# The order and the rate at which a hybrid mixer's projections are traced between its head chains

## The chip, the cores and the metric

One core of one Trainium2 chip runs the whole program. The metric is the device time in microseconds (us) of one execution; lower is better. The engines are named PE (TensorE, the matrix engine), DVE (VectorE), ACT (ScalarE), POOL (GpSimd) and SP (SyncE, which here only issues DMAs).

## The reference

A trunk of two layers over 512 positions of width 1024. Each layer is a SwiGLU feed-forward block (FFN) at half weight, a mixer, and a second FFN, each with a norm before and after and with shift, scale and gate from a conditioning vector. The mixer, the part that matters here, is:

```python
def hybrid_mixer(h, w_in, ...):
    proj = h @ w_in                                   # q, k, v, z, beta, a, u
    qkv = silu(causal_dwconv(qkv, conv_w))            # 4 taps along the sequence
    q, k = l2_normalize(heads(q)), l2_normalize(heads(k))
    o = chunked_gated_delta_rule(q, k, v, beta, g)    # 4 heads of 128, chunks of 64
    y_gdn = rms_norm(o, gdn_norm_w) * silu(z)
    y_s5 = s5_mixer(u, ...)                           # diagonal complex scan, 32 groups of 16 channels
    return concatenate([y_gdn, y_s5]) @ w_out

def chunked_gated_delta_rule(...):                    # per head and chunk
    system = lower_triangular(kb @ k.T * decay) + I
    w_val, k_cum = solve(system, [vb, kb * exp(g)])
    attn = q @ k.T * decay
    # then over the chunks, in order:
    v_new = w_val - k_cum @ S;  o = q @ S + attn @ v_new;  S = S * exp(g_last) + k.T @ v_new

def s5_mixer(u, ...):
    x = scan(abar, bbar @ u)                          # complex, along the sequence
    y = gelu(Re(c @ x) + d * u)
    return y * sigmoid(y @ w_glu)
```

## The kernel before

The kernel is written in a tile framework: it is traced as a program of tile operations, and a scheduler puts each engine's instructions into one order, in which what was traced earlier has priority. Each engine then takes its instructions in that order and waits where an input is not there.

fp32 precision in the wide matmuls comes from splitting each operand into a high and a low part in a reduced type: weight `wh`, `wl` and activation `..hh`, `..hl`. Three matmuls (L266 to L268: high by high, high by low, low by high) make one product of 128 rows by 512 positions, 24 of them one projection of 128 columns. `Weights.get` hands out the weights in the order in which they are packed, and prepares those that are next: a DMA on SP of 128x1024 into one of four raw buffers, two casts on ACT (L223) for `wh`, two subtractions for `wl` on DVE (L231) or, for 10 of a mixer's 30 weights, on POOL. So the DMA of a weight waits until the low part of the fourth weight before it is made.

A mixer (`mixer`, L1165) projects heads 0 and 1 first (L1199 to L1219). Then three kinds of work are traced in an interleaved way:

- `main1` (L1293) yields the projections that are left, in the order of the string `ORDER` (L48): `u` is the input of S5 (four groups of 24 matmuls, `m0u0` to `m0u3`, copied to `utc`, 16 steps), `2` and `3` are q, k, v of heads 2 and 3 (`m0p20` to `m0p32`, 12 steps each), each followed by its convolution over four taps (`conv`: one ACT copy, three DVE operations, SiLU on ACT). A step is 6 matmuls. The host packs the weights by the same string.
- `main2` (L1299) follows: z of the four heads (16 steps, `m0z0` to `m0z3`), then, when all of S5's outputs are traced, its gate matmuls (`m0gl0` to `m0gl3`), and, when the first heads' outputs are traced, the output projection (`m0od`).
- The chains: the decay factors (`gen_decay`), two head pairs (`gen_pair`: pair 0 is heads 0 and 1, pair 1 heads 2 and 3) and three S5 generators (`gen_s5`, four channel groups s0 to s3, the last by whichever is free first).

Names in the chains: `pu` and `pa` are the products k k^T and q k^T of a head (L941), `U` and `at` what ACT and DVE make of them, `g0` and `g1` the solve of pair 0 and pair 1. A solve is 15 forward substitution steps on DVE (L1004 shuffle, L1005 multiply, L1006 add, over `xs` and `xb`), for blocks of 16, and then merges of blocks on PE (`pp`, `px`, `pt`), with transposes on DVE (L1015, L1032) and copies on ACT between them. `pk` uses the solved block, `pb` are the matmuls of the recurrence over chunks, `S` the state (L1156 on DVE), `pon` the transposes of the heads' outputs. In S5 `vr` and `vi` are the input products, L849 to L854 and L860, L863 the products and the scans on DVE, `y` the output matmuls.

The loop at the end of `mixer` (L1349 on) sets how they are interleaved: in each round every active chain is advanced by one yield, and the projections by the number of steps that the table in L1357 adds to `acc`: nine in `main1`, one in `main2` until the fourth z is traced, two after it. Pair 1 joins the chains when v of head 2 has been traced (`(2 * started, 2) in qkv`).

Of the kernel before, what the change touches and what calls it, by code (L numbers as in the profile page):

```python
# [44 lines left out]
C_BD = 640  # L45
C_BS = 672
C_LV = 704
ORDER = "2u3"  # L48
C_GM = 736
C_E = C_GM + 2  # L50
NCST = C_E + BASE
# [3 lines left out]
def trunk(ctx: ExitStack, tc: tile.TileContext, x_d, c, wmod, wun, vecs, wab, s5p, cst_d, out, depth=2):  # L55
# [1113 lines left out]
    def mixer(l, h):  # L1169
# [87 lines left out]
        zs = [None] * 4  # L1257
# [7 lines left out]
        def main_u():  # L1265
            wu = [W.get(3 - i) for i in range(4)]
            tt = [slot(f"{name}utc{ch}") for ch in range(4)]
            for t in range(4):
                pu = mmps(f"{name}u{t}")
                for k in range(KD):  # L1270
                    hi, lo = wu[k // 2][0][k % 2], wu[k // 2][1][k % 2]
                    ht = [hh[:, t:T:4] for hh in h[k]]
                    PE.matmul(pu, ht[0], hi, start=k == 0, stop=False)
                    PE.matmul(pu, ht[1], hi, start=False, stop=False)
                    PE.matmul(pu, ht[0], lo, start=False, stop=k == KD - 1)
                    if k % 2:
                        yield
                for ch in range(4):
                    ACT.copy(tt[ch].rearrange("p (a t h) -> p t a h", a=8, t=4)[:, t],
                             q4(pu)[:, ch].rearrange("p (a h) -> p a h", a=8))  # L1280
            utc[:] = tt

        def main_qkv(hd):
            for i in range(3):
                w = W.get(3)
                ps = mmps(f"{name}p{hd}{i}")
                for k in range(KD):
                    mm3(ps, w, k, h[k], FULL, k == 0, k == KD - 1)
                    if k % 2:
                        yield  # L1290
                qkv[hd, i] = conv(slot(f"{name}c{hd}{i}"), ps, 4 * i + hd)

        def main1():  # L1293
            for i in ORDER:
                yield from main_u() if i == "u" else main_qkv(int(i))
# [52 lines left out]
        m1, m2 = main1(), main2()  # L1348
        active = [gen_decay(gates, decs, name, wait), mk(0), *s5]  # L1349
        m = m1  # L1350
        started = 1
        done, acc = object(), 0.0
        while active or m is not None:
            for c in list(active):
                if next(c, done) is done:
                    active.remove(c)
            acc += (9,1,2)[0 if m is m1 else 1 if zs[3] is None else 2]  # L1357
            while acc >= 1:
                acc -= 1
                if m is not None and next(m, done) is done:  # L1360
                    m = m2 if m is m1 else None
            while started < 2 and (2 * started, 2) in qkv:
                active.append(mk(started))
                started += 1
# [141 lines left out]
    for l in range(depth):  # L1506
        if l:
            spread(40, mod=(gen_mod(l, range(32, 72)), 40))
        h = ff(l, 0, h)
        drain()  # L1510
        h = mixer(l, h)
        if l + 1 < depth:
            load_vec(l + 1)
            spread(40, mod=(gen_mod(l + 1, range(32)), 32), prep=(gen_prep(l + 1), NPREP))
        h = ff(l, 2, h)
        drain()
# [6 lines left out]
def pack(inp):  # L1523
# [9 lines left out]
    def mt(w, m):  # L1533
        return w[:, m * P:(m + 1) * P].reshape(KD, P, P).transpose(1, 0, 2).reshape(P, 1024)
# [21 lines left out]
    for l in range(L):  # L1556
        u = ffu(f["ff1_w_in"][l], f["ff1_w_out"][l], head=l == 0)
        wm = f["mix_w_in"][l]
        for hd in range(2):
            u += [mt(wm, i * 4 + hd) for i in range(3)]  # L1560
        for hd in ORDER:
            if hd != "u":
# [58 lines left out]
```

## Time and profile before

| | |
|---|---|
| median of three runs | 2141.8 us |
| lowest and highest | 2138.74 and 2143.5 us |
| the profiled execution's own time | 2140.54 us |
| its span, first to last instruction | 2138.7 us |
| mean granted clock of PE | 0.971 |
| busy: PE, DVE, ACT, POOL | 95%, 59%, 41%, 25% |
| PE busy tenths in 40 slices of the span | 7999899999789999999999999999996899999998 |
| granted clock in tenths, same slices | 9999999999889999999999999999997899999999 |

Reading it: a slice of the last two rows is 53.5 us. The clock of PE has two levels, 2.4 and 1.2 GHz; a granted clock of 1.00 means the upper for the whole stretch, 0.75 half of the time at the lower. Slices 11 and 12 (535 to 642 us) lie in the first mixer, 31 and 32 (1604 to 1711 us) in the second. In the trace a name loses its buffer number (`m0p20` reads `m0p`), and `m0` and `m1` are the mixers of layers 0 and 1. A matmul's row gives the time from its start to its end; rows overlap, so the spacing of starts is what one costs.

### The profile page before, as it was taken

What the parts mean: (1) busy time and instruction counts of PE and PEld (TensorE: products, weight loads), DVE (VectorE), ACT (ScalarE), POOL (GpSimd) and SP (SyncE); (2) the same over time, 40 slices, a digit from 0 to 9 for tenths busy, and PEclk for the clock granted to TensorE, in tenths of its full rate; (3) what the DMA queues carried; (4) which work ended last, traced back from release to release, by engine and by line L of the source; (5) the groups of instructions that cost most, each with busy time, mean ns of one, the idle gap of its engine ahead of it and who ended that gap; (6) DMA issues with size and microseconds to landing.
All of it is one profiled execution on the core that took longest, in us unless ns stands there. A gap on an engine that the chain in (4) does not pass through costs nothing. (4 is left out here: it accounts for less than half of the span.)

```text
span 2138.7 us, 30816 instructions
## 1 busy us (share of the span) xinstructions
PE 2034.7 (95%) x11094; PEld 1725.4 (81%) x11094; DVE 1272.1 (59%) x3064; ACT 882.3 (41%) x1980; POOL 529.5 (25%) x941
## 2 busy tenths in 40 slices
PE   7999899999789999999999999999996899999998
PEld 5788688799667888888889888888985779888886
DVE  7956658764867835555574456558459486324235
ACT  4532313566256723222363232236653665323132
POOL 3147685112331016675010000001123300000001
PEclk9999999999889999999999999999997899999999
DMA  7686667405212235556433545542133022224231
GB/s 257 193 304 191 224 196 215 139 30 168 67 62 63 93 115 176 180 178 188 142 95 124 166 158 189 185 138 80 60 128 101 29 89 90 87 93 136 70 99 50
DMA packets 109694, 286.00 MB, mean 134 GB/s; under 512 B 31154, under 2 KB 32738, under 8 KB 109540
## 3 DMA queue, kind: packets, MB, share of 16 engines
q1 hardware_dynamic: 108388, 282.39, 41.2%
q8 instruction: 87, 1.43, 0.3%
q10 hardware_dynamic: 1152, 1.64, 0.2%
q14 instruction: 67, 0.55, 0.1%
HBM read 267.57 MB, written 16.41 MB: 133 GB/s over the span
## 5 line engine op out<-in xcount | busy, mean ns | idle before, releaser
L231 DVE TENSOR_TENSOR wl<-w,wh 128x512 fp32r<-128x512 f32 x608 | 412.3, 731 | 111.6 <-ACT wh L223 110.4
L223 ACT CAST wh<-w 128x512 fp32r<-128x512 f32 x648 | 357.0, 618 | 92.0 <-DMA w<-in_wun 53.7
L143 DVE SCALAR_TENSOR_TENSOR wm<-wm,cb 128x1024 f32<-128x1024 f32 x128 | 160.2, 1252 | 220.6 <-DMA wm<-in_wmod 220.4
L266 PE MATMUL f10i<-f02ohh,wh 128*128 128x512 f32 (+1 forms) x416 | 150.4, 362 | 1.5 <-DVE f02pt L324 1.3
L267 PE MATMUL f10i<-f02ohl,wh 128*128 128x512 f32 (+1 forms) x416 | 149.4, 359 | 2.3 <-ACT f02ohl L404 2.3
L266 PE MATMUL f02i<-m0ohh,wh 128*128 128x512 f32 (+1 forms) x416 | 148.8, 360 | 1.1 <-ACT f02sg L497 0.8
L268 PE MATMUL f10i<-f02ohh,wl 128*128 128x512 f32 (+1 forms) x416 | 149.3, 359 | 0.0
L266 PE MATMUL f12i<-m1ohh,wh 128*128 128x512 f32 (+1 forms) x416 | 148.2, 358 | 0.8 <-ACT f12sg L497 0.8
L267 PE MATMUL f12i<-m1ohl,wh 128*128 128x512 f32 (+1 forms) x416 | 148.1, 357 | 0.6 <-ACT m1ohl L404 0.6
L267 PE MATMUL f02i<-m0ohl,wh 128*128 128x512 f32 (+1 forms) x416 | 148.1, 357 | 0.6 <-ACT m0ohl L404 0.6
L268 PE MATMUL f12i<-m1ohh,wl 128*128 128x512 f32 (+1 forms) x416 | 147.9, 357 | 0.2 <-DVE wl L231 0.2
L268 PE MATMUL f02i<-m0ohh,wl 128*128 128x512 f32 (+1 forms) x416 | 147.9, 357 | 0.2 <-DVE wl L231 0.2
L267 PE MATMUL f00i<-h0l,wh 128*128 128x512 f32 x344 | 135.8, 395 | 4.9 <-DVE h0l L1477 4.9
L268 PE MATMUL f00i<-h0h,wl 128*128 128x512 f32 x344 | 135.4, 394 | 0.0
L266 PE MATMUL f00i<-h0h,wh 128*128 128x512 f32 x344 | 132.4, 393 | 0.2 <-ACT h0h L1472 0.2
L330 POOL TENSOR_TENSOR f12pt<-f12pt,Gr 128x512 f32<-128x512 f32 x8 | 10.5, 1315 | 406.0 <-ACT scr L329 406.0
L330 POOL TENSOR_TENSOR f10pt<-f10pt,Gr 128x512 f32<-128x512 f32 x8 | 10.7, 1340 | 361.1 <-ACT scr L329 357.3
L498 DVE TENSOR_TENSOR f12sg<-f12sg,f12i 128x512 f32<-128x512 f32 (+1 forms) x26 | 15.7, 606 | 136.8 <-PE f12i L268 120.8
L231 POOL TENSOR_TENSOR wl<-w,wh 128x512 fp32r<-128x512 f32 x40 | 52.3, 1328 | 170.0 <-ACT wh L223 157.4
L267 PEld LDWEIGHTS f10i<-f02ohl,wh 128*128 128x128 f32 x416 | 79.7, 192 | 13.7 <-ACT f02ohl L404 2.5
L266 PEld LDWEIGHTS f10i<-f02ohh,wh 128*128 128x128 f32 x416 | 79.6, 191 | 13.4 <-DVE f02pt L324 1.6
L266 PEld LDWEIGHTS f02i<-m0ohh,wh 128*128 128x128 f32 x416 | 78.3, 189 | 13.1 <-ACT f02sg L497 1.0
(2627 smaller groups left out, 5316.7 us busy)
## 6 DMA issues: line engine op xcount, KB each, us to landing
w<-in_wun SPq DMA_DIRECT2D x324, 512.0 KB, 4.0
wm<-in_wmod SPq DMA_DIRECT2D x128, 512.0 KB, 4.3
wm<-in_wmod SPq DMA_DIRECT2D x32, 256.0 KB, 6.0
s5d<-zero SPq DMA_DIRECT2D x4, 1280.0 KB, 13.2
Gr<-Gd SPq DMA_DIRECT2D x12, 256.0 KB, 3.2
x<-in_x SPq DMA_DIRECT2D x4, 512.0 KB, 5.5
m0s0tb<-s5d SPq DMA_DIRECT2D x7, 256.0 KB, 4.7
m0s1tb<-s5d SPq DMA_DIRECT2D x7, 256.0 KB, 3.4
```

The lines of the kernel that those rows point to most:

```text
L143: DVE.scalar_tensor_tensor(w, w, 1.0, cb, op0=ALU.mult, op1=ALU.mult, accum_out=m)
L223: ACT.copy(hi[j], raw[:, j * T:j * T + T])
L231: e.tensor_tensor(lo[j], raw[:, j * T:j * T + T], hi[j].bitcast(F32), op=ALU.subtract)
L266: PE.matmul(ps, hi, h[0][:, sl], start=start, stop=False)
L267: PE.matmul(ps, hi, h[1][:, sl], start=False, stop=False)
L268: mark["pe"] = PE.matmul(ps, lo, h[0][:, sl], start=False, stop=stop)
L330: (POOL if self.part else DVE).tensor_tensor(y, src, self.G[dh], op=ALU.mult)
L498: DVE.tensor_tensor(sg, sg, pu[:, :n], op=ALU.mult)
```

## The change

Two lines: the string that orders the projections of `main1` and the packing of their weights, and the table of steps per round.

```diff
--- before.py
+++ after.py
@@ -45,7 +45,7 @@
 C_BD = 640
 C_BS = 672
 C_LV = 704
-ORDER = "2u3"
+ORDER = "u23"
 C_GM = 736
 C_E = C_GM + 2
 NCST = C_E + BASE
@@ -1354,7 +1354,7 @@
             for c in list(active):
                 if next(c, done) is done:
                     active.remove(c)
-            acc += (9,1,2)[0 if m is m1 else 1 if zs[3] is None else 2]
+            acc += (2,1,1)[0 if m is m1 else 1 if zs[3] is None else 2]
             while acc >= 1:
                 acc -= 1
                 if m is not None and next(m, done) is done:
```

The packing, the count of operations and the arithmetic are otherwise the same. Where the instructions stand then is decided by the scheduler. Three places follow, in mixer 0.

PE around the product k k^T of pair 0 (`m0h0pu`, `m0h1pu`): before, in the middle of the z projections.

```order
L268 MATMUL m0z_5417<-f00ohh_4056,wl_1_5242 128x512
L266 MATMUL m0z_5417<-f00ohh_4058,wh_1_5238 128x512
L267 MATMUL m0z_5417<-f00ohl_4059,wh_1_5238 128x512
L268 MATMUL m0z_5417<-f00ohh_4058,wl_1_5242 128x512
L941 MATMUL m0h0pu<-m0c_4447 128x128 x4
L941 MATMUL m0h1pu<-m0c_4574 128x128 x4
L845 MATMUL m0s0vr<-m0s0U,m0s0tb_5315 128x128 x4
L847 MATMUL m0s0vi<-m0s0U,m0s0tb_5317 128x128 x4
```

After, the same two rows stand among the matmuls of `m0u`.

```order
L1273 MATMUL m0u_4965<-wh_1_4873,f00ohh_4058 128x512
L1274 MATMUL m0u_4965<-wh_1_4873,f00ohl_4059 128x512
L1275 MATMUL m0u_4965<-wl_1_4877,f00ohh_4058 128x512
L941 MATMUL m0h0pu<-m0c_4447 128x128 x4
L941 MATMUL m0h1pu<-m0c_4574 128x128 x4
L1273 MATMUL m0u_5007<-wh_0_4862,f00ohh_4052 128x512
L1274 MATMUL m0u_5007<-wh_0_4862,f00ohl_4053 128x512
L1275 MATMUL m0u_5007<-wl_0_4866,f00ohh_4052 128x512
```

They moved from behind all the projections of `main1` and the first of z to behind three quarters of u.

PE around the first merge of pair 1's solve (`m0g1pp`): before, between gate matmuls, with pair 0's merge not yet done (`m0g0pt`).

```order
L268 MATMUL m0gl_6536<-m0s1yh,wl_0_5799 128x512
L1049 MATMUL m0g0px_6150<-m0g0cu,m0g0cx 32x32 x15
L266 MATMUL m0gl_6536<-m0s2yh,wh_0_5795 128x512
L267 MATMUL m0gl_6536<-m0s2yl,wh_0_5795 128x512
L268 MATMUL m0gl_6536<-m0s2yh,wl_0_5799 128x512
L1024 MATMUL m0g1pp_6181<-m0g1cx,m0g1cu 32x32 x32
L1057 MATMUL m0g0pt_6221<-cst,m0g0X_6086 64x64 x8
L935 MATMUL m0h0tv<-cst,m0c_4453 128x128 x4
L935 MATMUL m0h1tv<-cst,m0c_4580 128x128 x4
```

After, pair 0's outputs (`m0h0pon`, `m0h1pon`) stand around it.

```order
L266 MATMUL m0gl_6722<-m0s3yh,wh_0_6303 128x512
L267 MATMUL m0gl_6722<-m0s3yl,wh_0_6303 128x512
L268 MATMUL m0gl_6722<-m0s3yh,wl_0_6307 128x512
L1119 MATMUL m0h0pon_6409<-cst,m0h0o 128x128 x2
L1024 MATMUL m0g1pp_6415<-m0g1cx,m0g1cu 32x32 x32
L1119 MATMUL m0h1pon_6468<-cst,m0h1o 128x128 x2
L1030 MATMUL m0g1px_6474<-m0g1cu,m0g1cx 32x32 x32
L1042 MATMUL m0g1pp_6521<-m0g1cx,m0h2U 32x32 x8
L1042 MATMUL m0g1pp_6521<-m0g1cx,m0h3U 32x32 x8
L1049 MATMUL m0g1px_6546<-m0g1cu,m0g1cx 32x32 x16
```

Pair 0 is at its end when pair 1's solve is merged, where before both were in the solve.

DVE in the last part of pair 1's solve (`m0g1xs`, `m0g1xb`): before, S5's last group (`m0s3t`) stands in it.

```order
L849 TENSOR_TENSOR m0s3t_6015<-m0s3tb_5945,m0s3vr 128x512
L1005 TENSOR_TENSOR m0g1xs<-m0g1xs,m0g1uc 128x8x13
L850 TENSOR_TENSOR m0s3t_6018<-m0s3tb_5947,m0s3vr 128x512
L851 TENSOR_TENSOR m0s3t_6016<-m0s3tb_5947,m0s3vi 128x512
L852 TENSOR_TENSOR m0s3t_6017<-m0s3tb_5945,m0s3vi 128x512
L1031 TENSOR_TENSOR m0g0cu<-m0g0cu,m0g0px_6051 128x256
L854 TENSOR_TENSOR m0s3t_6015<-m0s3t_6015,m0s3t_6016 128x512
L1032 STREAM_TRANSPOSE m0g0cx<-m0g0cu 128x256
L1006 TENSOR_TENSOR m0g1xb<-m0g1xb,m0g1xs 128x8x13
L860 SCALAR_TENSOR_TENSOR m0s3t_6016<-r_899,m0s3t_6015 128x128 x4
L863 SCALAR_TENSOR_TENSOR m0s3t_6018<-r_899,m0s3t_6017 128x128 x4
L1004 STREAM_SHUFFLE m0g1xs<-m0g1xb 128x8x14
```

After, at the solve's beginning, pair 0's states and outputs stand around it (`m0h0S`, `m0h0o`, and `m0z`, which takes the output's transpose `m0h0pon`).

```order
L1156 SCALAR_TENSOR_TENSOR m0h0S_6223<-m0h0S_6093,m0geg,m0h0pb_6173 128x128
L1156 SCALAR_TENSOR_TENSOR m0h1S_6232<-m0h1S_6102,m0geg,m0h1pb_6178 128x128
L1160 TENSOR_TENSOR m0h0o<-m0h0o_6225,m0h0pb_6173 128x128
L1001 COPY m0g1xb<-cst 128x128
L1123 SCALAR_TENSOR_TENSOR m0z_6154<-m0h0pon_6282,vec_122,m0z_6154 128x256
L1160 TENSOR_TENSOR m0h1o<-m0h1o_6234,m0h1pb_6178 128x128
L1004 STREAM_SHUFFLE m0g1xs<-m0g1xb 128x8
L1005 TENSOR_TENSOR m0g1xs<-m0g1xs,m0g1uc 128x8
L1125 TENSOR_TENSOR m0h0yl<-m0z_6154,m0h0yh 128x256
L1006 TENSOR_TENSOR m0g1xb<-m0g1xb,m0g1xs 128x8
L1004 STREAM_SHUFFLE m0g1xs<-m0g1xb 128x8x2
```

S5's scans have gone out of pair 1's solve, and pair 0's recurrence has come in.

## Rows read from the trace of the kernel before

**Rows 1.** The page, busy time: us, share of the span, instructions.
```profile
PE 2034.7 (95%) x11094; PEld 1725.4 (81%) x11094; DVE 1272.1 (59%) x3064; ACT 882.3 (41%) x1980; POOL 529.5 (25%) x941
```

**Rows 2.** PE timeline: start us, length us, line, output<-inputs, shape, count [idle before].
```profile
467.81 0.50 PE L266 MATMUL m0p<-f00ohh,wh 128*128 128x512 f32 x1
...
531.04 0.39 PE L266 MATMUL m0z<-f00ohh,wh 128*128 128x512 f32 x1
...
536.48 1.05 PE L941 MATMUL m0h0pu<-m0c 128*128 128x128 f32 x8
...
538.26 1.06 PE L845 MATMUL m0s0vr<-m0s0U,m0s0tb 128*128 128x128 f32 x8
...
715.09 0.67 PE L266 MATMUL f02i<-m0ohh,wh 128*128 128x256 f32 x3
...
1512.24 0.50 PE L266 MATMUL m1p<-f10ohh,wh 128*128 128x512 f32 x1
...
1763.18 0.70 PE L266 MATMUL f12i<-m1ohh,wh 128*128 128x256 f32 x3
```

**Rows 3.** PE's waits, 467 to 716: us in total, times, longest us.
```profile
PE m0s1y L880 <- ACT m0h3U L977: 8.0, 1, 8.0
PE m0h2pa L941 <- DVE m0h0at L992: 5.2, 1, 5.2
PE m0g1pp L1024 <- DVE m0g1cx L1015: 4.3, 1, 4.3
PE m0g0pp L1042 <- DVE m0g0cx L1032: 4.2, 1, 4.2
```

**Rows 4.** PE's waits, 1512 to 1764, first and last of 11.
```profile
PE m1s1y L880 <- ACT m1h3U L977: 7.8, 1, 7.8
...
PE m1g1pp L1076 <- ACT m1h2vb L1071: 0.3, 1, 0.3
```

**Rows 5.** Windows: PE, PEld, DVE, ACT, POOL busy us, granted clock, DMA share, GB/s.
```profile
500.00:520.00 20.00, 20.00 (x91) 18.72 (x91) 6.64 (x22) 15.43 (x60) 2.84 (x2) 1.00 0.47 156
520.00:540.00 20.00, 20.00 (x112) 17.29 (x111) 7.20 (x10) 9.12 (x20) 7.64 (x6) 1.00 0.58 192
...
560.00:580.00 20.00, 12.33 (x66) 10.78 (x64) 20.00 (x51) 1.14 (x4) 11.35 (x12) 0.83 0.46 144
580.00:600.00 20.00, 13.92 (x137) 12.24 (x138) 18.66 (x88) 13.39 (x26) 4.28 (x4) 0.74 0.35 120
600.00:620.00 20.00, 11.82 (x163) 8.52 (x162) 19.37 (x54) 5.39 (x11) 7.35 (x8) 0.72 0.10 27
```

**Rows 6.** DVE timeline, from S5's first product to pair 1's solve.
```profile
544.25 0.68 DVE L849 TENSOR_TENSOR m0s0t<-m0s0tb,m0s0vr 128x512 f32<-128x512 f32 x1
544.85 0.28 DVE L986 TENSOR_TENSOR m0g0uc<-m0g0cx 128x128 f32<-128x128 f32 x1
...
600.30 0.22 DVE L1005 TENSOR_TENSOR m0g1xs<-m0g1xs,m0g1uc 128x64 f32<-128x64 f32 x1
...
604.27 0.01 DVE L1004 LOAD_MASK_SELECT m0g1xs<-m0g1xb  x1
...
610.22 2.44 DVE L860 TENSOR_TENSOR_SCAN m0s3t<-r,m0s3t 128x128 f32<-128x128 f32 x4
...
614.91 0.01 DVE L1004 LOAD_MASK_SELECT m0g1xs<-m0g1xb  x1
...
619.79 0.45 DVE L1015 STREAM_TRANSPOSE m0g1cx<-m0g1cu 128x256 f32<-128x256 f32 x1
```

**Rows 7.** PE timeline, first matmuls after waits and first merges of both solves.
```profile
567.26 2.07 PE L941 MATMUL m0h2pa<-m0c,m0c 128*128 128x128 f32 x8 [5.16 <-DVE m0h0at L992]
...
595.71 0.75 PE L1024 MATMUL m0g0pp<-m0g0cx,m0g0cu 32*32 32x32 f32 x64
...
620.38 1.08 PE L1024 MATMUL m0g1pp<-m0g1cx,m0g1cu 32*32 32x32 f32 x64 [4.32 <-DVE m0g1cx L1015]
```

**Rows 8.** Tile `m0h2pk` on PE: count, ns min/median/max, first and last start us.
```profile
L941 PE MATMUL m0h2pk<-m0h2X,m0h2kc x8: 273/275/275, 651.5 to 652.3; 128*128 128x128 f32 x8
```

## The prediction, made before the changed kernel ran

> **What bounds the kernel now.** I read the page's busy line first: TensorE (PE) is busy 95% of the span [rows 1], so a change of order can only win idle time of PE, or time at its lower clock. The two mixers are where that idle time sits. I then read PE's timeline from the first matmul after the gates' transposes, 467.81, to the first matmul of the next FFN, 715.09 [rows 2]: 247.3 us for mixer 0. The same two places in mixer 1, 1512.2 and 1763.2, stand 250.9 us apart.
>
> What would PE need there without a wait and at full rate? Prices come from the same timeline. The 24 wide matmuls of one z step group run from 531.04 to 536.48, 0.227 us each; two groups of eight fp32 products run from 536.48 to 538.26, 0.111 each [rows 2]. With 588 wide matmuls (134 us), 392 products (44 us), and transposes and the small matmuls of the two solves at the spacing of their own undisturbed rows (29 us), I estimate 207 us. So mixer 0 loses 40.5 us and mixer 1 44.
>
> The view of PE's waits splits that loss. In mixer 0 its 13 rows sum to 26.1 us, of which four make up 21.7: for `m0h3U`, `m0h0at` and twice for a transpose in the solve of a head pair [rows 3]. In mixer 1 the 11 rows sum to 27.4 [rows 4]. What is left, 14.4 and 16.7 us, is work at a lower clock. The windows show it: the granted clock is 1.00 to 540 and 0.83, 0.74, 0.72 in the three stretches from 560 to 620 [rows 5].
>
> The cause is the vector engine (DVE). In the same windows it is busy 20.00, 18.66 and 19.37 of 20 us from 560 to 620, but 6.64 and 7.20 from 500 to 540 [rows 5]. The mixer's projections run first and leave DVE slack; then the S5 scans and both 15-step solves come at once, from 544.25 to 619.79 [rows 6], 75.5 us on one engine, while PE has little left that needs none of it.
>
> **The change part by part.** The set of operations is the same, save for one more load of an activation table in each mixer's ScalarE (ACT) order. What moves is where projections stand between the chains.
>
> *Pair 0 and S5 go forward.* Before, 24 matmuls of z and all projections stand ahead of pair 0's `pu`: 68.4 us of PE work by the prices above. After, 72 of u's matmuls and the chains' transposes do: 22.2 us. So the DVE work of pair 0 and S5 begins some 46 us earlier, with 68 us of wide matmuls (rest of u, heads 2 and 3, z, the gate's gl0 to gl2) and some 49 us of the chains' own small ones between that `pu` and pair 1's solve result `g1pp` at 139.6. Those 117 us of PE work face the 75.5 us of DVE work plus the DVE work that already stood in 480 to 540, 28.3 us by the windows (two of the three are shown [rows 5]); head 2 and 3's convolutions are in it. 104 in 117: it fits, but DVE has no room to wait in.
>
> It does wait, since each engine takes its instructions in the order they stand. I walked the order from 467.8, giving each instruction the duration of its row of before, and starting it when its inputs and its engine are free. PE then loses: 2.8 us at head 2's first projection, whose weight's high half stands behind the U copies on ACT; 7 at the third projection of head 3 (`p32`), whose PSUM bank is freed by a convolution that stands on DVE behind S5's products; 2.9 and 1 around pair 0's solve; 4.5 at z2 and S5's last group, where PE waits for head 3's convolution and for ACT. The sum is 18.2. These are bounded by 0, if DVE keeps ahead, and by the 21.7 that the four large waits of now take [rows 3].
>
> *Pair 1 goes back.* Its `pu` needs head 3's convolutions, and those now come after u. From its `pu` to its `g1pp` stand only 22.1 us of PE work. What the chain takes is bounded by its solve: four steps and two thirds from 600.30 to 604.27, with little between, are 0.85 us each, so 15 steps are 13 us; with the 8.4 us from pair 0's `pu` [rows 2] to its solve operand `m0g0uc` at 544.85 [rows 6] that is 21, the lower end. The upper is pair 0 now, from 536.48 [rows 2] to 595.71 [rows 7], 59.2 us amid S5's scans. In the new DVE order pair 0's output steps (state S, o and its norm) stand between the solve's steps. They are short beside S5's: by the walk 31.7 us, nearer the lower end, so PE waits 9.6 us at `g1pp`.
>
> *The tail.* From `g1pp` to the products `h2pk` the trace has 620.38 [rows 7] to 651.5 [rows 8], 31.1 us, with pair 0's work and the gate between; the new order holds 12.8 us of PE work there. The chain's own operations, with the copies on ACT that stand ahead of each other, come to 19.7 by the walk: 6.9 lost, between 0 and 18.3. The recurrence that follows loses 1.5 more (0 to 3), as its outputs now end later against the output projection, which finishes at 207 of PE work either way.
>
> *The clock.* After the wait of 5.16 us the eight products of `m0h2pa` took 2.07 us [rows 7], where pair 0's `pu` took 1.05 [rows 2]; the second group beside it did the same, so such a wait costs some 2 us more. The new order has two waits above 5 us (`p32`, `g1pp`): 4 us, between 0 and the 14.4 of now.
>
> *Weights and tables.* Weight loads keep their number, and DMA is idle for most of the stretch. The tables of S5 are asked for sooner, on the sync engine's queue behind the weights of u. That is 0 to 2 us per mixer; I take 0, since S5's first use stands at 40 us of PE work.
>
> **The sum.** 18.2 + 9.6 + 6.9 + 1.5 + 4 = 40.2 us lost per mixer, against 40.5 and 44.1: a gain of 0.3 and 3.9, 4.2 together; the extra table loads (two of 1.28 us on ACT) stay within the walk's waits. The profiled execution took 2140.54 us, 1.3 below the median of the three runs. 2140.5 - 4.2 = 2136.3, which I round to 2136. The answer is a small difference of large terms, and the range says so.
>
> **The rivals.** *The cover is ample.* If DVE keeps ahead in the shared stretch, PE loses some 4 us there and not 18.2. For it: DVE's 104 in 117 us. Against: the three engines' fixed orders. Then 26 us are lost per mixer, a gain of 14.5 and 18.1: 2108.
>
> *Pair 1 is left alone at the end (slower).* Its solve stands on DVE behind and between pair 0's state steps, and each of those waits for PE and ACT, which wait in turn for weights and for z's activations. Now such a crossing can be seen in the trace: between two halves of pair 1's solve steps stand the S5 scans, from 610.22 to 614.91, 4.7 us for eight instructions that the solve does not need [rows 6]. If pair 1 takes halfway between the walk's 31.7 and pair 0's 59.2, some 43 to 45 us, PE waits 12 us more per mixer: 2136 + 24 = 2160. It decides from 37 us on: 5 us more per mixer are 10 in all, which is 2146, at the edge of what can be told from no change. For it: nothing on PE is left to fill with, since u, heads 2, 3 and z are spent. Against: by then S5 is nearly done. The Trainium skill, PSUM — Partial Sum Buffer, section "Engine vs sequencer instructions", says the queues of ScalarE, VectorE and GpSimd are strictly first in, first out, so a solve step behind a waiting state step cannot pass it. The scans in the solve's midst agree with it; by that rule alone the time leans to this rival's 2160 and not to 2108.
>
> *The tables or weights come late.* S5's first products then wait 2 to 5 us per mixer: 2140 to 2146. *It does not do what it says*: excluded, as the order of PE shows pair 0's `pu` behind u alone.
>
> **How the numbers follow.** About 0.2%, 4.3 us, is what can be told from no change, so "same" is 2137.5 to 2146.1. The forecast has 0.42, with 8 us either way from its terms: 0.24 faster, 0.17 same, 0.01 slower. The ample cover has 0.23, all faster. Pair 1 alone has 0.30, all slower. Late tables have 0.05: 0.04 same, 0.01 slower. So faster 0.47, same 0.21, slower 0.32. The likeliest's own range is 2128 to 2144; the range over all reaches from 2111, leaving out the better half of the ample cover, to 2160, leaving out the worse third of the slow rival.
>
> **What would show it.** In the new trace, pair 0's `pu` near 490, and granted clock 1.00 until about 537. Right: PE's largest wait at `g1pp` with DVE as the releaser, 8 to 12 us, beginning near 625; 560 to 600 with PE above 17 of 20 us. Ample cover: no wait above 3 us before 600. Slow rival: `g1pp` later than 643 in mixer 0, and a granted clock under 0.8 after it. The prediction is wrong as a whole if PE loses time in a stretch outside the mixers.

## The result, and the profile after

The changed kernel takes 2154.2 us (2153.02 to 2155.24, four runs) beside 2141.97 for the kernel before on the same chip: a ratio of 1.0058, interval 1.0043 to 1.0073. It is slower by 12 us, where 2136 was forecast. A second time, beside other runs of before, it gave 1.0041 (1.0026 to 1.0056); the loss is 8 to 12 us by these two. Both mixers are longer: 255.0 and 254.5 us from their first matmul to the next FFN's first, against 247.3 and 250.9 [rows 2]. The work between and behind the mixers takes what it took.

The page of the changed kernel, its span, busy time and granted clock, which answer to [rows 1]:

```profile
span 2151.2 us, 30828 instructions
...
PE 2043.5 (95%) x11094; PEld 1728.7 (80%) x11094; DVE 1265.7 (59%) x3064; ACT 882.1 (41%) x1982; POOL 528.8 (25%) x941
...
PEclk9999999999988999999999999999999799999999
```

PE is busy for 9 us more with the same matmuls. In the clock's row the slices below 9 are now the 12th and 13th, 592 to 699 us, and the 32nd; before they were the 11th and 12th, 535 to 642, and the 31st and 32nd. The low stretch has moved back in the mixer.

PE's waits in mixer 0 (us in total, times, longest), which answer to [rows 3]:

```profile
PE m0g1pp L1024 <- DVE m0g1cx L1015: 4.6, 1, 4.6
PE m0h0pon L1119 <- DVE m0h0o L1112: 4.4, 1, 4.4
PE m0p L266 <- DVE m0c L1179: 4.4, 1, 4.4
PE m0h0pb L1139 <- DVE m0h0S L1152: 3.9, 1, 3.9
PE m0h2pon L1119 <- DVE m0h2o L1112: 1.8, 2, 1.5
...
```

The waits of 8.0 and 5.2 us are gone. In their place stand four of about 4 us and a tail of small ones, 29.2 us in 17 rows of the mixer against 26.1 in 13. So PE waits 3 us more than before; the other 5 of mixer 0 are work that takes longer. The first two of these rows lie back to back, from the end of a gate matmul at 632.3 to the first merge at 642.04, with only two transposes between them.

The windows of mixer 0's second half (PE, PEld, DVE, ACT, POOL busy us; then granted clock, DMA share, GB/s), which answer to [rows 5], and two shorter ones at these two waits:

```profile
580.00:600.00 20.00, 14.14 (x99) 12.35 (x99) 16.60 (x27) 9.21 (x24) 9.36 (x10) 1.00 0.38 128
600.00:620.00 20.00, 19.27 (x118) 16.78 (x118) 11.25 (x41) 14.98 (x47) 1.47 (x2) 0.91 0.02 6
620.00:640.00 20.00, 12.77 (x69) 10.27 (x69) 17.50 (x83) 7.64 (x25) 8.21 (x9) 0.87 0.26 79
640.00:660.00 20.00, 14.30 (x242) 11.61 (x242) 4.67 (x13) 10.91 (x26) 2.73 (x3) 0.50 0.01 2
660.00:680.00 20.00, 19.93 (x118) 16.68 (x117) 11.28 (x29) 12.42 (x38) 8.54 (x8) 0.87 0.17 54
...
630.00:635.00 5.00, 2.30 (x11) 1.56 (x9) 4.78 (x31) 1.48 (x6) 2.36 (x4) 0.97 0.31 81
635.00:640.00 5.00, 0.69 (x2) 0.29 (x2) 4.73 (x26) 0.40 (x1) 0.00 (x0) 0.50 0.13 55
```

Before, DVE was full and the clock low from 560 to 620. Now DVE is busy for 5 of the 20 us from 640 to 660, and the clock is 0.50, the lower level, for all of it. It was there from 635 on, in the first of the two waits, before the first merge. What PE has from 642 to 656 are pair 1's merges and some transposes; then seven matmuls of the gate follow, at the lower clock too.

The same mixer along PE's timeline. The rows are, in this order: first matmul, pair 0's `pu`, pair 1's `pu`, the transpose between the two waits, pair 1's first merge, the end of its third, the gate matmul that stands between, its last merge, `pk`, the next FFN.

```profile
469.25 0.63 PE L1273 MATMUL m0u<-wh,f00ohh 128*128 128x512 f32 x1
...
492.06 1.05 PE L941 MATMUL m0h0pu<-m0c 128*128 128x128 f32 x8
...
608.16 1.06 PE L941 MATMUL m0h2pu<-m0c 128*128 128x128 f32 x8
...
636.75 0.69 PE L1119 MATMUL m0h0pon<-cst,m0h0o 128*128 128x128 f32 x2 [4.45 <-DVE m0h0o L1112]
642.04 1.08 PE L1024 MATMUL m0g1pp<-m0g1cx,m0g1cu 32*32 32x32 f32 x64 [4.60 <-DVE m0g1cx L1015]
...
654.41 1.06 PE L1076 MATMUL m0g1pp<-m0g1Z,m0h3U 64*64 64x64 f32 x8
656.68 0.80 PE L266 MATMUL m0gl<-m0s0yh,wh 128*128 128x512 f32 x1 [1.21 <-ACT m0z L1308]
...
659.96 1.97 PE L1086 MATMUL m0g1px<-m0g1X,m0g1Z 64*64 64x64 f32 x16
...
663.31 1.91 PE L941 MATMUL m0h2pk<-m0h2X,m0h2kc 128*128 128x128 f32 x8
...
724.29 0.40 PE L266 MATMUL f02i<-m0ohh,wh 128*128 128x256 f32 x2
```

### The profile page after: what moved, and what is told of

It reads as the page before. It is cut to its first block, busy times and chain, and to the rows that moved or that the text cites. A ratio compares the mean times of both kernels' runs of the same rounds, so it can differ in the third digit from the quotient of the medians.

```text
span 2151.2 us, 30828 instructions
## 1 busy us (share of the span) xinstructions
PE 2043.5 (95%) x11094; PEld 1728.7 (80%) x11094; DVE 1265.7 (59%) x3064; ACT 882.1 (41%) x1982; POOL 528.8 (25%) x941
## 4 chain that ended last, share of the span: by engine, by line
PE 59%; DVE 13%; ACT 6%; issue 3%; DMA 1%; POOL 0%; SPq 0%; DVEq 0%; ACTq 0%; POOLq 0%
PE f10i L266 4%; PE f10i L268 4%; PE f10i L267 4%; PE f12i L268 3%; PE f12i L266 3%; PE f12i L267 3%; PE f02i L266 3%; PE f02i L268 3%; PE f02i L267 3%; DVE wl L231 1%; PE f12o L274 1%; PE f10o L274 1%; PE f02o L273 1%; PE f12o L275 1%; PE f10o L275 1%
## 5 line engine op out<-in xcount | busy, mean ns | idle before, releaser
L266 PEld LDWEIGHTS f10i<-f02ohh,wh 128*128 128x128 f32 x416 | 79.8, 192 | 13.4 <-DVE f02pt L324 1.8
L266 PEld LDWEIGHTS f12i<-m1ohh,wh 128*128 128x128 f32 x416 | 78.3, 189 | 12.8 <-ACT f12sg L497 1.0
```

Source lines behind the costliest of these rows:

```text
L266: PE.matmul(ps, hi, h[0][:, sl], start=start, stop=False)
```

## Experiments: which of the two edits

**Order alone.** The string of the change, the table of before.

```diff
-ORDER = "2u3"
+ORDER = "u23"
```

> ORDER is "u23", the table stays (9,1,2). If the rate is the cause, pair 1 still meets pair 0 in the solve: its first merge stands at 125 us of PE work in the mixer (120 before, 140 in the changed kernel), so the time is that of before, 2138 to 2148. If the order of u and the heads is the cause, it is that of the changed kernel, 2150 to 2158.

2145.96 us median of ten runs, ratio 1.0013 (1.0002 to 1.0024). Its mixers take 250.9 and 250.5 us. The order by itself costs 3 us.

**Rate alone.** The table of the change, the string of before.

```diff
-            acc += (9,1,2)[0 if m is m1 else 1 if zs[3] is None else 2]
+            acc += (2,1,1)[0 if m is m1 else 1 if zs[3] is None else 2]
```

> ORDER stays "2u3", the table is (2,1,1). Pair 1's first merge stands at 140 us of PE work in the mixer, as in the changed kernel. If the rate is the cause: 2150 to 2158, with a granted clock of 0.5 for 20 us or more after pair 1's first merge. If the order is the cause: 2138 to 2148.

2152.09 us, ratio 1.0042 (1.0030 to 1.0054): the changed kernel's loss without its order. Its mixers take 254.7 and 254.5 us, and pair 1's first merge (tile view: count, ns, first and last start) stands where it stands in the changed kernel:

```profile
L1024 PE MATMUL m0g1pp<-m0g1cx,m0g1cu x64: 191/191/212, 643.4 to 644.0; 32*32 32x32 f32 x64
```

The granted clock is 0.50 from 650 to 665 in this run, and 0.61 and 0.84 in the 5 us on either side, as was expected if the rate is the cause. The merge is 172.8 us into the mixer, as in the changed kernel; before it was 152.6 [rows 2, 7]. The rate moved it, and by its first number, as the run that follows leaves that number alone and has the merge as late (174 us into the mixer).

**The third number alone, put back.**

```diff
-            acc += (2,1,1)[0 if m is m1 else 1 if zs[3] is None else 2]
+            acc += (2,1,2)[0 if m is m1 else 1 if zs[3] is None else 2]
```

> "u23" with (2,1,2): only the last number of the changed table goes back. Up to pair 1's first merge the order of PE is that of the changed kernel; the output projection's first matmuls now stand ahead of pair 1's last outputs. If the loss lies at pair 1's merges the time stays within 3 us of the changed kernel: 2151 to 2157. If it lies in the recurrence behind them, some 3 to 6 us a mixer come back: 2142 to 2148.

2147.72 us median of ten runs, ratio 1.0024 (1.0012 to 1.0037), so 4 to 7 us come back, as the second theory said. The order of PE is the same up to pair 1's merges; after them the output projection's matmuls now lie among the recurrence, and the wait of 1.8 us for pair 1's outputs is 0.4. The profiled run is the longest of the ten (2151.8), with mixers of 255.9 and 253.1 us, so the traces do not show where the medians' gain lies. It is clear of noise beside the first ratio of the changed kernel (1.0058, from 1.0043) and not beside the second (1.0041, from 1.0026).

With the order alone these medians make a ladder for the order `u23`: 1.0013 with (9,1,2), 1.0024 with (2,1,2), 1.0041 and 1.0058 with (2,1,1). So the order costs some 3 us, the first number, which moves pair 1's first merge from 158 to 174 us into the mixer, some 2 more that are not clear of noise, and the third number, which lets the output projection come later, 4 to 7: the largest part of the loss by these medians. (9,1,1) was not run, so whether the third number costs as much without the first is open.

**The changed kernel again**, beside other runs of before:

> The changed kernel once more, on the chip and beside the runs of before that the other kernels of this call share: 2151 to 2157 by every theory.

2151.52 us, ratio 1.0041; mixers of 254.7 and 253.7 us. A mixer differs by a microsecond or two from one execution to the next, so the medians decide and the traces say where.

**Pair 1 forward at the slow rate.** If pair 1 being late is the loss, heads 2 and 3 ahead of u should mend it.

```diff
-ORDER = "u23"
+ORDER = "23u"
```

> ORDER "23u" with the changed table (2,1,1): the same slow rate, but heads 2 and 3 ahead of u, so pair 1's first merge stands at 102 us of PE work and not at 140, and S5's first output at 117 and not at 74. If pair 1's place at the end is the cause of the loss, the time falls to 2125 to 2143. If a slow rate costs by itself (chains that wait for each other on the in-order engines), or S5 now stands at the end in pair 1's place, it stays at 2148 to 2160.

2155.78 us, ratio 1.0057 (1.0039 to 1.0074): no gain. Pair 1's first merge did come early, at 111.6 us into the mixer and 61 us sooner than in the changed kernel, but its `pk`, at 170, only 24 us sooner, and S5's last output moved back from 136 to 185 us. PE's three largest waits (4.8, 4.4 and 3.9 us) are in pair 1's chain, all for DVE; ahead of the first of them DVE has S5's scans and products. So it is not pair 1's start as such. That at this rate some chain always ends alone is how we read it, and is not shown; three orders were run at it.

**The same at a rate of three.**

```diff
-            acc += (2,1,1)[0 if m is m1 else 1 if zs[3] is None else 2]
+            acc += (3,1,1)[0 if m is m1 else 1 if zs[3] is None else 2]
```

> ORDER "23u" with (3,1,1): pair 1's first merge at 117 us of PE work (120 before), S5's last output at 143, z earlier than with a rate of two. If the place of pair 1's merges decides, the time is near before or below, 2128 to 2144; if S5 at the end takes their place, 2146 to 2158.

2166.38 us, ratio 1.0109 (1.0094 to 1.0124), worse than all others and above both ranges that were expected. Its largest waits are 8.0 us for pair 0's X and 6.0 for pair 0's second merge, both on DVE. Why three is worse than two was not followed further.

## Experiments: what makes the tail long

**Matmuls into the waits, to keep the clock up.** Five fp32 matmuls of constants in each of two waits of about 4.5 us, at low priority so that they stand last of what is ready (for `pp0` of pair 1 likewise):

```diff
+                if n and not pr and not i:
+                    with tc.high_priority(-400):
+                        for _ in range(5):
+                            PE.matmul(pt, ident, cst[:, 0:T], start=True, stop=True)
```

> The changed kernel with ten more fp32 matmuls (512 columns, constants, into PSUM banks that are overwritten after) in each mixer: five where PE waits 4.4 us for pair 0's last output transpose, five where it waits 4.6 us for pair 1's first merge. They cost PE about 9 us in each mixer, all in its waits; nothing else moves. If the clock is what makes pair 1's merges slow, they now run at a granted clock near 1.0 and 6 to 10 us come back in each mixer: 2134 to 2143. If the merges are held by the copies and multiplications between them on ACT and DVE, the clock rises and the time stays: 2149 to 2156.

2153.43 us, ratio 1.0045: nothing gained. But the test was half a test, as its windows show (columns as above):

```profile
635.00:640.00 5.00, 4.85 (x15) 2.17 (x14) 4.81 (x32) 0.00 (x0) 0.05 (x1) 1.00 0.35 103
640.00:645.00 5.00, 3.54 (x71) 1.59 (x69) 3.85 (x13) 0.81 (x2) 0.00 (x0) 1.00 0.01 2
645.00:650.00 5.00, 3.00 (x128) 2.68 (x128) 1.06 (x3) 2.33 (x6) 0.00 (x0) 0.60 0.01 3
650.00:655.00 5.00, 4.42 (x34) 3.84 (x30) 0.83 (x2) 2.18 (x5) 0.00 (x0) 0.50 0.00 0
```

The clock stays at 1.00 through the filled waits and falls to 0.50 after the merges have begun to run by themselves.

**The same within the merges.** More such matmuls ahead of the merges' own, sized to PE's waits there.

```diff
+        FILL = {"px0": (T, T), "pp1": (T,), "px1": (HT,), "pt2": (HT,), "pp2": (T,)}
+                for c in FILL.get(n, ()) if pr else ():
+                    PE.matmul(ps[:, :c], ident, cst[:, 0:c], start=True, stop=True)
```

> The kernel of e3_fill, which left the granted clock at 0.50 from 647 to 666 us, with further fp32 matmuls of constants where PE waits inside pair 1's merges: 1.8 us before the second product, 0.9 before the third, 0.4 before each of the next two, 0.9 before the one after. If the lower clock is what makes the merges 24 us long, they now run at the upper one, pair 1's pk stands 4 to 6 us closer to its first merge, and 2143 to 2149 is the time. If the copies and products on ACT and DVE between them make it, the clock rises, PE waits longer instead, and the time is 2151 to 2156.

2150.66 us, ratio 1.0036 (1.0024 to 1.0049), beside 1.0041 for the changed kernel measured together with it: 1 us at best, with intervals that overlap. The median lies between the two ranges that were expected, next to the second. Now the clock did stay up to the end of the third merge:

```profile
640.00:645.00 5.00, 5.00 (x117) 2.92 (x117) 1.50 (x4) 2.33 (x6) 0.00 (x0) 1.00 0.01 3
645.00:650.00 5.00, 4.46 (x69) 3.29 (x67) 0.83 (x2) 2.56 (x7) 0.00 (x0) 1.00 0.00 0
650.00:655.00 5.00, 2.65 (x6) 2.15 (x7) 0.00 (x0) 4.96 (x12) 2.06 (x2) 0.63 0.02 3
```

And this is what PE did with it: first merge, third merge's end, the gate matmul that stands between, last merge, `pk`.

```profile
638.20 0.75 PE L1035 MATMUL m0g1pp<-m0g1cx,m0g1cu 32*32 32x32 f32 x64
...
648.83 0.63 PE L1087 MATMUL m0g1pp<-m0g1Z,m0h3U 64*64 64x64 f32 x8
652.35 0.79 PE L266 MATMUL m0gl<-m0s0yh,wh 128*128 128x512 f32 x1 [2.89 <-ACT m0z L1323]
...
655.63 1.97 PE L1097 MATMUL m0g1px<-m0g1X,m0g1Z 64*64 64x64 f32 x16
...
658.97 1.27 PE L941 MATMUL m0h2pk<-m0h2X,m0h2kc 128*128 128x128 f32 x5
```

The third merge is over 11.3 us after the first began, against 13.4 in the changed kernel. Then PE waits 2.9 us for ACT, where 1.2 were waited before, and the last merge begins 17.4 us after the first, against 17.9. The clock's gain turned into a wait for ACT. That is the second theory, and the timelines of the changed kernel show why. ACT (start, us, line, output<-input, count):

```profile
651.70 0.58 ACT L1060 COPY m0g1Z<-m0g1pt 64x512 f32<-64x512 f32 x1 [3.69 <-PE m0g1pt L1057]
652.30 0.82 ACT L1065 COPY m0h2X<-m0g1X 64x256 f32<-64x256 f32 x2
653.13 0.82 ACT L1065 COPY m0h3X<-m0g1X 64x256 f32<-64x256 f32 x2
653.96 1.14 ACT L1071 ACTIVATE m0h2vb<-m0h2tv,m0g1ir 128x128 f32<-128x128 f32 x4
654.98 1.16 ACT L1071 ACTIVATE m0h3vb<-m0h3tv,m0g1ir 128x128 f32<-128x128 f32 x4
655.98 0.65 ACT L1308 ACTIVATE m0z<-m0z 128x512 f32<-128x512 f32 x1
656.46 1.20 ACT L223 CAST wh<-w 128x512 fp32r<-128x512 f32 x2
657.67 0.58 ACT L1077 COPY m0g1Z<-m0g1pp 64x512 f32<-64x512 f32 x1
```

The third merge ends on PE at 655.47, but the copy of its result (`m0g1Z` from `m0g1pp`) starts at 657.67: ahead of it on ACT stand the copies of X, eight scalings of v, the SiLU of the last z and two weight casts, and the last three are still to do. The Trainium skill, PSUM — Partial Sum Buffer, section "Engine vs sequencer instructions", says that ScalarE's queue is strictly first in, first out, and the rows agree: an input that was ready waited 2.2 us. The copy is over at 658.25 and the last merge begins at 659.96; these further 1.7 us are PE's own order, in which seven gate matmuls stand ahead of it. DVE meanwhile (in brackets, the idle time and what ended it):

```profile
649.23 0.87 DVE L1051 TENSOR_SCALAR m0g1X<-m0g1px 32x256 f32<-32x256 f32 x2 [3.26 <-PE m0g1px L1049]
661.97 0.42 DVE L1088 TENSOR_SCALAR m0h2X<-m0g1px 64x256 f32<-64x256 f32 x1 [11.87 <-PE m0g1px L1086]
```

**Twelve of the copies on DVE.** For pair 1, the copies into X and the scalings of v go from ACT to DVE.

```diff
-                ACT.copy(q4(X[i])[b, :, b], x4[b, 4 * i:4 * i + 4])
+                (DVE.tensor_copy if pr else ACT.copy)(q4(X[i])[b, :, b], x4[b, 4 * i:4 * i + 4])
-                ACT.activation(q4(vb[i])[:, c], q4(tv)[:, c], AF.Copy, scale=ir[:, 4 * i + c:4 * i + c + 1])
+                if pr:
+                    DVE.tensor_scalar(q4(vb[i])[:, c], q4(tv)[:, c], ir[:, 4 * i + c:4 * i + c + 1], None, op0=ALU.mult)
+                else:
+                    ACT.activation(q4(vb[i])[:, c], q4(tv)[:, c], AF.Copy, scale=ir[:, 4 * i + c:4 * i + c + 1])
```

> The changed kernel with twelve of pair 1's copies (two of each X, four of each vb) on DVE, which is idle for 11.9 us there, and not on ACT, where they stand 3.9 us long between the two copies of Z. If ACT's order holds pair 1's merges, its last product (px of L1086) comes 3 to 4 us sooner after the first merge, and 6 to 8 us come back in all: 2143 to 2147 beside 2151.5 for the changed kernel. If PE's clock or the recurrence behind decides, less than 2 us: 2149 to 2153.

2148.1 us median of ten runs, ratio 1.0022 (1.0012 to 1.0031). First merge, end of the third merge, last merge, `pk` on PE:

```profile
640.67 1.07 PE L1024 MATMUL m0g1pp<-m0g1cx,m0g1cu 32*32 32x32 f32 x64 [4.61 <-DVE m0g1cx L1015]
...
653.01 1.06 PE L1079 MATMUL m0g1pp<-m0g1Z,m0h3U 64*64 64x64 f32 x8
654.74 1.96 PE L1089 MATMUL m0g1px<-m0g1X,m0g1Z 64*64 64x64 f32 x16 [0.67 <-ACT m0g1Z L1080]
...
660.45 0.72 PE L941 MATMUL m0h2pk<-m0h2X,m0h2kc 128*128 128x128 f32 x5
```

The last merge begins 14.1 us after the first, against 17.9: 3.8 us sooner, as expected. The edit did more than take twelve operations off ACT: with them gone, the scheduler also put the SiLU of z and the two casts behind the copy of Z, and the gate matmuls behind the last merge. The 3.8 us are the 2.2 of the late copy and most of the 1.7 of the gate matmuls. `pk` gains only 1.5 of them (19.8 against 21.3), as the gate matmuls now stand between the last merge and `pk`, at the lower clock. In all 3.4 us came back beside the later of the changed kernel's two times (2151.5), where 6 to 8 were expected. The time lies above the range for ACT's order and below that for the clock, so it does not decide; the rows show ACT's order at the last merge.

**Both together.**

> The same copies on DVE, in the kernel of e5_fill_merges, which keeps the clock up until pair 1's merges are nearly over and gained nothing by it, or 1 us. If ACT hid what the clock gave, both together gain more than each: another 2 to 3 us a mixer, 2137 to 2143. If the clock is of no weight: as e9, 2143 to 2147.

2144.36 us median of ten runs, ratio 1.0012 (1.0002 to 1.0021). The same rows:

```profile
640.51 0.75 PE L1035 MATMUL m0g1pp<-m0g1cx,m0g1cu 32*32 32x32 f32 x64
...
652.43 1.14 PE L1100 MATMUL m0g1px<-m0g1X,m0g1Z 64*64 64x64 f32 x16 [0.67 <-ACT m0g1Z L1091]
...
657.81 0.38 PE L941 MATMUL m0h2pk<-m0h2X,m0h2kc 128*128 128x128 f32 x1 [1.95 <-POOL m0h2kc L1095]
```

The last merge begins 11.9 us after the first. With ACT out of the way the clock is worth 2 us there, where alone it was worth 0.5; the next to be late is POOL's multiplication for `pk`. 2144.4 is 1 us above what was expected for this theory and within what was expected for the other, so the median alone would not tell them apart; the rows do.

**And the third number.** All of the tail's remedies in the changed kernel: the copies, the matmuls in the waits, and (2,1,2).

> The kernel of e10_copies_and_fill with the third number of the table back at 2, as in e4_third_two. If the output projection's place (e4) and pair 1's merges (e10) are separate losses of the tail, their gains add: 4 to 6 us on top of e10's 2144, 2137 to 2141, and the loss of the changed kernel beside before is all in its tail. If both give back the same microseconds: 2142 to 2146.

2139.91 us median of ten runs, ratio 0.9985 (0.9975 to 0.9995). The gains add: beside 1.0041 the copies with the matmuls gave 0.0029 of the ratio and the third number 0.0017, which makes 0.0046, and 0.0056 were measured. With its tail mended the changed kernel is level with the kernel before, or a little below, although its front is as it was: pair 0 first, and the 4.6 us wait for head 3's convolution still there.

**The copies in the kernel before**, for both pairs (`True` for `pr`):

> The kernel before with the same copies on DVE, for both pairs. There pair 0's and pair 1's merges lie beside gate matmuls, S5's last output and each other, and DVE is busy for 3.8 of 20 us (620 to 640). If ACT holds the merges there too (it was busy 14.2 of these 20 us), 2 to 4 us a mixer come back: 2135 to 2139 beside 2143 for before. If other work covers them: within 2 us of before.

2138.42 us, ratio 0.9972 (0.9960 to 0.9983): 4 us faster than before, and the fastest kernel of this study. The time is the one expected if ACT holds the merges; the trace does not show it there, as from pair 1's first merge to `pk` mixer 0 takes 32.1 us, against 31.1 before.

This run bears on the cause. The copies on DVE give 4 us in the kernel before, there for both pairs, and 3.4 in the changed one by its later time, so with them in both the changed kernel is as far behind as without (1.0022 against 0.9972, beside 1.0041 and 1.0058). ACT's order is a cost of both kernels and not what sets them apart. With all remedies, against before with the copies, the distance is 0.9985 to 0.9972, about what the order alone costs; the matmuls in the waits were not tried in the kernel before.

## Why the prediction was wrong, by its own steps

The sum was a walk along the mixer, so it can be read at its stations. Loss so far is time into mixer 0 less PE's work up to there, by the prices of the prediction; the forecast's 4 us of clock are put half to `pu`, half to the first merge.

| station | PE work | forecast loss | measured at | measured loss |
|---|---|---|---|---|
| pair 1's `pu` | 117.5 | 20.2 | 138.9 | 21.4 |
| its first merge | 139.6 | 31.8 | 172.8 | 33.2 |
| its `pk` | 150.6 | 38.7 | 194.1 | 43.5 |
| end | 206.8 | 40.2 | 255.0 | 48.2 |

The 150.6 is counted back from the end, by the matmuls that stand behind `pk`. The prediction's own 12.8 us from the first merge would put `pk` at 152.4; then 41.7 us are lost up to it and 6.5 behind it.

**Up to the first merge the sum was right, its parts were not.** Pair 0's `pu` ran at 492 where some 490 was forecast. From pair 1's `pu` to its first merge it took 33.9 us where the walk had 31.7. But the waits ahead of pair 1's `pu` are 14.0 us and not 18.2: 4.4 and not 7 at `p32`, 0.8 and not 2.8 at head 2's first projection, and 1.4 for a table of S5 (`m0s0vr` for the DMA of `m0s0tb`), which the prediction had put at 0. The other 7.4 us lost there are in no wait, where 2 were put for the clock. The 9.6 us at `g1pp` came as two waits, 4.4 for pair 0's outputs and 4.6 for the transpose, so the sign that was named, 8 to 12 us at `g1pp`, did not come, nor did PE above 17 of 20 us to 600 (14.1 in the last 20). That the sums agree to 1.4 us is in part luck. The first merge, at 642.0, is just short of the 643 that the slow rival named as its own, so the rival's mechanism, a solve stretched to 43 us and more, did not come about either. What it argued with did: little stood beside pair 1, and its second sign came, a clock under 0.8 behind the first merge (0.50).

**The failed step is the tail, and in it the clock.** From the first merge to `pk` the walk lost 6.9 us and the kernel 10.3 (8.5 by the prediction's own count); behind it the walk lost 1.5 and the kernel 4.7 (6.5), outside the 0 to 3 that were given. That is 6.6 of the 8.0 us by which mixer 0 missed its forecast of 247.0; the two mixers make 15.5 of the 16.7 us between 2136.3 and the profiled 2153.0, and 1.4 are a later start of the first mixer, which differs from run to run. Of the 15.0 us that the kernel lost behind the first merge only 5.4 are waits; the other 9.6 are in no wait, most of it work at the granted clock of 0.50, and the walk had nothing for the clock in its tail. It took each row's duration of before, where pair 1's merges ran mostly at the upper level: its last merge took 1.14 us there, in the row that follows, and 1.97 in the changed kernel.

```profile
646.91 1.14 PE L1086 MATMUL m0g1px<-m0g1X,m0g1Z 64*64 64x64 f32 x16
```

The prediction put the clock at 4 us, with a bound of 14.4, by counting waits above 5 us. There was none above 4.6 us, and yet 19 us of the mixer's loss are in no wait, and 29 in waits where 36 were forecast. The clock was at 0.50 from 635, where PE stood in the first of two waits of 4.4 and 4.6 us that lie back to back, and it stayed there through the merges. The waits alone do not decide it: with them filled by matmuls it was 1.00 up to 645 and 0.60 and 0.50 in the merges that follow. The prediction did name "the copies on ACT that stand ahead of each other", and its bounds of 0 to 18.3 for that term held.

**Waits and clock are not two terms.** The prediction added them. The runs with matmuls in the waits raised the clock and the time stayed, since ACT then set the pace; with ACT relieved the same clock was worth more. The expectation of the first such run, made by adding, was 6 to 10 us a mixer from the clock alone.

**The comparison was weak at the other end too.** The prediction found losses of 40.5 and 44 us in the two mixers of before, and forecast a gain of 4 from the difference to 40.2. A difference of that size, of a sum of five walked terms, had no firm sign; it gave "slower" a chance of 0.32 and should have given it more, since the largest term of the tail was set near the lower of its two bounds.

**What the change was up against.** The gain that was to come, pair 0 and S5 under the projections, did come: the waits of 8.0 and 5.2 us are gone. It was spent again at the end. Before, the two solves and S5 stand together in the middle, at a bad clock, but behind them the gate, pair 0's and pair 1's recurrences and the output projection cover each other: from the end of pair 1's first merges on, little is idle, and the clock is 1.00 from 640:

```profile
640.00:660.00 20.00, 18.69 (x147) 16.25 (x146) 10.67 (x31) 18.17 (x54) 6.34 (x6) 1.00 0.17 53
```

After the change pair 0 is finished when pair 1 begins to merge, and in this order nothing but a part of the gate stands beside it. Work is left: all 192 matmuls of the output projection stand behind `pk`, and 144 of them read only outputs of S5 and of pair 0. No run moved them ahead of the merges; the run with the third number at 2 moved some of them ahead of pair 1's last output transposes.

## What to carry to other kernels

In this kernel, bringing one chain forward under cover took the cover from the chain that comes last, and letting the output projection come later cost at least as much. Before such a change, write down what each engine still has to do beside the last chain, and price its serial part with small matmuls at the lower clock and with each in-order engine's own queue, not at the prices of a busy stretch. Where an idle engine lies beside a full one in that stretch, moving some copies there was worth as much here (4 us, in the kernel before) as the order of the projections cost by itself (3 us).

## What the runs showed of the hardware

A busy PE did not mean a granted clock of 1.00. Two windows of the changed kernel, with columns as above: from 650 to 655 PE is busy for all 5 us, with 64x64 merges and transposes, at 0.50; before it, at the same 0.50, it was busy for half.

```profile
645.00:650.00 5.00, 2.73 (x67) 2.36 (x68) 1.67 (x5) 2.33 (x6) 0.00 (x0) 0.50 0.01 3
650.00:655.00 5.00, 5.00 (x38) 4.55 (x37) 0.10 (x1) 3.23 (x10) 0.00 (x0) 0.50 0.00 0
```

The same merges with 512-column matmuls between them ran at 1.00, as the windows of the kernel with matmuls in the merges show. An fp32 matmul of 128x128 by 512 columns took 0.89 us (five of them 4.45 us in the first filled wait, where the trace counts ten), and ten of them in the waits of a mixer lengthened nothing that could be told: ratio 1.0045, between the two of the changed kernel. And four scalings of 128x128 from PSUM took 1.13 us on DVE, in the row that follows, and 1.14 on ACT, in the timeline above, so that such copies can go to whichever engine is free.

```profile
651.36 1.13 DVE L1072 TENSOR_SCALAR m0h2vb<-m0h2tv,m0g1ir 128x128 f32<-128x128 f32 x4 [1.43 <-PE m0h2tv L935]
```
